# Gates and branch products with the activations stationary, runs of equal matmuls, and a transposed x and memory from the host, in a two-layer encoder

## The chip, the cores and the metric

The kernel runs on one core of one Trainium2 chip. The metric is the device time of one execution in microseconds (us), the median of the runs.

## The reference

Two post-norm layers on 256 tokens of width 1024, in fp32. One input projection of each token gives the parts of three attention branches (latent attention with low-rank queries and keys, differential attention, attention into 256 memory tokens) and three gates:

```python
h = x @ w_in[l]
c_q, c_kv, k_pe, dq, dk, dv, mq, gate_pre = jnp.split(h, splits, axis=-1)
o_mla = _mla_branch(...); o_diff = _diff_branch(...); o_mem = _mem_branch(mq, mem, mem_w_kv[l])
g = jax.nn.sigmoid(gate_pre.reshape(b, s, N_BRANCH, d) + b_gate[l])
merged = (g[:, :, 0] * (o_mla @ wb[:512]) + g[:, :, 1] * (o_diff @ wb[512:1536])
          + g[:, :, 2] * (o_mem @ wb[1536:]))
x = _layernorm(DEEPNORM_ALPHA * x + merged @ w_out[l], ln1_g[l], ln1_b[l])
f = jnp.square(jax.nn.relu(x @ mlp_w1[l])) @ mlp_w2[l]
x = _layernorm(DEEPNORM_ALPHA * x + f, ln2_g[l], ln2_b[l])
```

## The kernel before

Every fp32 operand of a product is kept as a high and a low part in a reduced fp32 format (`F32R`). `mm3` (L119) makes a product of three matmuls, high x high, high x low, low x high. Where the moving operand is short (256 tokens), `mm_wide` (L124) does it in two: one with the high weights, which moves the high and the low part of the activations together (2 x 256 columns, a "wide" step), and one with the low weights and the high activations (256 columns, a "narrow" step); it alternates them k by k. `wload` (L98) loads a weight tile into a ring of 6 raw buffers on SP's queue and splits it: a cast on ACT (L111, the high part) and a subtraction on DVE (L112, the low part) into a ring of 8 tiles (`whl`). `evac` (L136) does the same to a result in PSUM. PSUM has 8 banks: four under the name `acc`, four under `sm`.

At the start x is loaded with the tokens on the partitions, transposed by TensorE in blocks of 128 x 128 and split (`fill_xT`, L181), and then the first group of differential queries, keys and values is projected (`DiffProj.step`, L234). The memory is loaded and transposed likewise (`load_memT`, L278), once for each layer.

A layer is a list of steps in a string (`ORDER`, L52): P projects a differential group, D, M and A are attention heads of the three branches, L and U the latent path, T, K and Q memory and its queries; g, h, e are the gates of the memory, the differential and the latent branch, and G, H, E the branch products. A token such as `g0` advances that generator by one yield. A planner, which simulates the engines, then lays out the instructions of each engine, with the program's order as priority; it can pass an instruction that is not ready, and takes tiles from the rings as they come free.

`gate` (L650) computes 256 output features of one gate: two weight tiles, 128 features stationary, 256 tokens moving, 8 k x 3 matmuls for each 128 features into one half of an `acc` bank, then tanh on ACT with the bias as a per-partition scalar (L667). `branch` (L672) does the same for a branch product, with 4 or 8 k; its result is multiplied by the gate (L695, L697) and added to the merged sum (L698), and after the last branch the sum is split into the stationary tiles `mhl` of the product with w_out (L701, L702). So the merged sum is made with features on the partitions, as the product with w_out (L899) needs it. After w_out comes a layer norm, then the MLP: `mlp1` (L930, mm_wide) and the second product (`mlp2_mm`, L963, mm3 with the activations stationary and 512 columns of weights moving).

Of the kernel before, what the change touches and what calls it, by code (L numbers as in the profile page):

```python
# [17 lines left out]
P = 128  # L18
T = 256
# [24 lines left out]
BUFS = dict(raw=6, whl=8, whlx=4, att=12, o=6, pexp=4, natd=3, gt=4, fr=2, pT=2, sc=8)  # L44
# [15 lines left out]
def encoder_trunk(ctx: ExitStack, tc: tile.TileContext, x, mem, positions, w_in, b_gate,  # L60
                  q_norm, kv_norm, w_uq, w_ukv, lam, subln, w_mkv, w_branch, w_out,
                  ln1_g, ln1_b, w1, w2, ln2_g, ln2_b, inv, rows, out):
# [35 lines left out]
    def wload(src, a, b, ring="whl"):  # L98
# [25 lines left out]
    def mm_wide(ps, lh, ll, r2, first, last):  # L124

        if last:
            PE.matmul(ps[:, 0, :], lhsT=ll, rhs=r2[:, 0, :], start=False, stop=False)
        PE.matmul(ps, lhsT=lh, rhs=r2, start=first, stop=last)  # L128
        if not last:
            PE.matmul(ps[:, 0, :], lhsT=ll, rhs=r2[:, 0, :], start=False, stop=False)  # L130
# [69 lines left out]
    class DiffProj:  # L200
# [13 lines left out]
        def queries_keys(self, t, cs=range(4)):  # L214
# [4 lines left out]
            for c in cs:  # L219
                w = self.weights(0, c)  # L220
                for k in range(2 * c, 2 * c + 2):
                    xh, xl = xk(self.xT, k, t)
                    mm3(self.qk[t], xh, xl, w[0][:, k % 2], w[1][:, k % 2], k == 0, k == KD - 1)
# [819 lines left out]
```

## Time and profile before

| what | value |
|---|---|
| median of 3 runs | 1015.45 us (1015.1 to 1015.85) |
| the profiled execution | 1014.8 us |
| its span in the trace | 1013.0 us |
| matmuls on PE | 6277 |

The profile is of one execution. PE is TensorE's matmuls, PEld its weight loads, DVE, ACT and POOL the other engines, SP the engine that issues most DMAs; a "q" behind an engine's name is its sequencer, which issues DMAs. L120 is line 120 of the kernel. A group of instructions is named by line, engine, operation and tiles, out<-in. Matmuls are pipelined: each shows some 0.28 to 0.4 us, though the next starts much earlier, so the distance between two starts tells more than a duration. Idle time of an engine is given with what ended it.

### The profile page before, as it was taken

How to read it: one execution, taken by the hardware profiler on the slowest of the kernel's cores; microseconds unless marked ns; L12 is line 12 of the kernel's file. 1: busy time of each engine (PE TensorE's matmuls, PEld its weight loads, DVE VectorE, ACT ScalarE, POOL GpSimd, SP SyncE). 2: the span in 40 equal slices, each digit the busy share in tenths (PEclk: the TensorE clock that was granted, in tenths of full speed). 3: DMA queues.
4: the chain of work that ended last, by engine and by line, in shares of the span. 5: the costliest groups of instructions: out<-in, count | busy, mean ns of one | idle time of the engine just before them, and what ended most of it. 6: DMA issues, size and time to landing. Idle time of an engine off the chain costs nothing.

```text
span 1013.0 us, 16430 instructions
## 1 busy us (share of the span) xinstructions
PE 997.7 (98%) x6277; PEld 903.6 (89%) x6277; DVE 741.8 (73%) x1135; ACT 590.2 (58%) x1078; POOL 44.3 (4%) x86
## 2 busy tenths in 40 slices
PE   7999999999999999999999999999999999999997
PEld 6989899999998888888889989999999978888885
DVE  6868789677769776665776888887677876656664
ACT  6767777666564554444634877776665625444540
POOL 0101010000000000000000210000100000000000
PEclk9999999999999999999999999999999999999999
DMA  9776554545667366666754754455356725766631
GB/s 330 229 211 169 144 146 139 153 122 149 242 185 239 108 204 192 194 192 190 252 160 145 230 167 141 136 157 146 107 164 231 247 85 158 233 191 180 204 116 41
DMA packets 133258, 178.06 MB, mean 176 GB/s; under 512 B 6528, under 2 KB 115132, under 8 KB 133180
## 3 DMA queue, kind: packets, MB, share of 16 engines
q1 hardware_dynamic: 132203, 176.22, 57.1%
q8 instruction: 49, 0.80, 0.3%
q10 hardware_dynamic: 976, 0.80, 0.2%
q14 instruction: 30, 0.24, 0.1%
HBM read 174.89 MB, written 2.10 MB: 175 GB/s over the span
## 4 chain that ended last, share of the span: by engine, by line
PE 95%; DVE 2%; DMA 2%; ACT 1%; issue 1%; DVEq 0%; ACTq 0%
PE mlp1.sm L128 11%; PE branch.acc L121 6%; PE branch.acc L122 6%; PE branch.acc L120 6%; PE mlp2.acc L120 6%; PE mlp2.acc L122 6%; PE mlp2.acc L121 6%; PE mlp1.sm L130 5%; PE diff_proj.acc L120 5%; PE diff_proj.acc L121 5%; PE diff_proj.acc L122 5%; PE diff_att.sm L515 2%; PE mq.acc L128 1%; PE gate.acc L121 1%; PE gate.acc L120 1%; PE gate.acc L122 1%
## 5 line engine op out<-in xcount | busy, mean ns | idle before, releaser
L112 DVE TENSOR_TENSOR mlp1.whl<-mlp1.raw,mlp1.whl 128x1024 fp32r<-128x1024 f32 x124 | 150.9, 1224 | 86.7 <-ACT mlp1.whl L111 83.4
L111 ACT CAST mlp1.whl<-mlp1.raw 128x1024 fp32r<-128x1024 f32 x124 | 129.5, 1051 | 90.6 <-PE mlp2.acc L122 43.0
L128 PE MATMUL mlp1.sm<-wout.xT,mlp1.whl 128*128 128x512 f32 x480 | 167.0, 398 | 0.0
L130 PE MATMUL mlp1.sm<-wout.xT,mlp1.whl 128*128 128x256 f32 x420 | 117.8, 281 | 0.0
L128 PEld LDWEIGHTS mlp1.sm<-wout.xT,mlp1.whl 128*128 128x128 f32 x480 | 87.1, 188 | 16.8
L120 PE MATMUL mlp2.acc<-mlp1.whl,mlp1.att 128*128 128x512 f32 x240 | 93.5, 389 | 0.0
L122 PE MATMUL mlp2.acc<-mlp1.whl,mlp1.att 128*128 128x512 f32 x240 | 93.4, 389 | 0.0
L121 PE MATMUL mlp2.acc<-mlp1.whl,mlp1.att 128*128 128x512 f32 x240 | 93.4, 389 | 0.0
L112 DVE TENSOR_TENSOR branch.whl<-branch.raw,branch.whl 128x1024 fp32r<-128x1024 f32 x56 | 68.3, 1220 | 26.5 <-ACT branch.whl L111 26.1
L130 PEld LDWEIGHTS mlp1.sm<-wout.xT,mlp1.whl 128*128 128x128 f32 x420 | 79.3, 189 | 2.5
L111 ACT CAST branch.whl<-branch.raw 128x1024 fp32r<-128x1024 f32 x56 | 58.8, 1051 | 32.8 <-PE branch.acc L122 19.7
L112 DVE TENSOR_TENSOR diff_proj.whl<-diff_proj.raw,diff_proj.whl 128x1024 fp32r<-128x1024 f32 x51 | 62.1, 1219 | 14.2 <-ACT diff_proj.whl L111 13.9
L111 ACT CAST diff_proj.whl<-diff_proj.raw 128x1024 fp32r<-128x1024 f32 x51 | 53.9, 1061 | 17.6 <-PE diff_proj.acc L122 9.0
L533 ACT COPY mlp1.sum<-mlp1.sm 128x256 f32<-128x256 f32 x60 | 22.4, 373 | 57.6 <-PE mlp1.sm L128 57.6
L121 PEld LDWEIGHTS mlp2.acc<-mlp1.whl,mlp1.att 128*128 128x128 f32 x240 | 45.1, 188 | 9.5
L122 PEld LDWEIGHTS mlp2.acc<-mlp1.whl,mlp1.att 128*128 128x128 f32 x240 | 45.1, 188 | 9.4
L120 PEld LDWEIGHTS mlp2.acc<-mlp1.whl,mlp1.att 128*128 128x128 f32 x240 | 45.1, 188 | 8.8
L120 PE MATMUL diff_proj.acc<-diff_proj.whl,mlp1.xT 128*128 128x512 f32 (+1 forms) x128 | 44.1, 345 | 0.5 <-ACT mlp1.xT L138 0.5
L121 PE MATMUL diff_proj.acc<-diff_proj.whl,mlp1.xT 128*128 128x512 f32 (+1 forms) x128 | 43.3, 339 | 0.0
L122 PE MATMUL diff_proj.acc<-diff_proj.whl,mlp1.xT 128*128 128x256 f32 (+1 forms) x128 | 43.2, 341 | 0.0
L120 PE MATMUL diff_proj.acc<-diff_proj.whl,start.xT 128*128 128x512 f32 (+1 forms) x124 | 42.3, 343 | 0.0
L121 PE MATMUL diff_proj.acc<-diff_proj.whl,start.xT 128*128 128x256 f32 (+1 forms) x124 | 41.7, 339 | 0.1
(444 smaller groups left out, 2909.8 us busy)
## 6 DMA issues: line engine op xcount, KB each, us to landing
mlp1.raw<-in_mlp_w_dram SPq DMA_DIRECT2D x124, 512.0 KB, 4.5
branch.raw<-in_w_branch_dram SPq DMA_DIRECT2D x32, 512.0 KB, 3.5
diff_proj.raw<-in_w_in_dram SPq DMA_DIRECT2D x62, 256.0 KB, 3.3
branch.raw<-in_w_in_dram SPq DMA_DIRECT2D x24, 512.0 KB, 3.7
diff_proj.raw<-in_w_in_dram SPq DMA_DIRECT2D x20, 512.0 KB, 3.8
wout.raw<-in_w_out_dram SPq DMA_DIRECT2D x16, 512.0 KB, 3.6
gate.raw<-in_w_in_dram SPq DMA_DIRECT2D x12, 512.0 KB, 3.7
mem_keys.raw<-in_mem_w_kv_dram SPq DMA_DIRECT2D x8, 512.0 KB, 7.1
```

What stands on the lines that cost most here:

```text
L111: S.copy(out=hl[:, 0, :n], in_=raw[:, :n])
L112: V.tensor_tensor(hl[:, 1, :n], raw[:, :n], f32v(hl[:, 0, :n]), ALU.subtract)
L120: PE.matmul(ps, lhsT=lh, rhs=rh, start=start, stop=False)
L121: PE.matmul(ps, lhsT=lh, rhs=rl, start=False, stop=False)
L122: PE.matmul(ps, lhsT=ll, rhs=rh, start=False, stop=stop)
L128: PE.matmul(ps, lhsT=lh, rhs=r2, start=first, stop=last)
L130: PE.matmul(ps[:, 0, :], lhsT=ll, rhs=r2[:, 0, :], start=False, stop=False)
L515: PE.matmul(po[:, t * T:(t + 1) * T], lhsT=pT[:, hl, kt * T + t * P:kt * T + (t + 1) * P], rhs=vh[:, :, kt * T + j * P:kt * T + (j + 1) * ...
L533: S.copy(out=d, in_=ps[:, 1, :])
```

## The change

- `gate` and `branch` take 512 output columns (n = 0 or 1) instead of 256. The activations, 128 tokens at a time, are stationary and 512 columns of weights move; each uses two `acc` banks, one per token half, and one weight tile of two k and 512 columns per step. A gate has four steps (yields), a branch two (memory), four (differential) or two and a third for transposes (latent).
- The result has tokens on the partitions. So the gate's bias is loaded as a broadcast to all partitions into one of two buffers (on SP's queue, at the gate's first step) and added by DVE before the tanh, and the merged sum is transposed by TensorE and evacuated into `mhl`.
- `mm_wide` does a whole chain of eight k: four wide steps, eight narrow ones, four wide ones.
- The host hands in x and memory transposed too. x comes in five pieces on ACT's queue and is split from SBUF; each piece is followed by its steps of the first projection. Memory comes in two pieces with tiles of its own (`mT`).
- The order strings are new and differ for the two layers. Three pairs of gate tiles instead of four single ones.

```diff
+    "L0 T0 L0 P0 Q0 P0 K0 L0 K0 D0 K0 D0 Q0 M0 M1 P1 M0 D0 P1 M0 P2 M0 P1 D0 D0 M1 D0 P1 M1 P2 U0 P2 U0 "
+    "M1 D1 P2 D0 D1 P3 e0 P3 D1 D2 P3 D1 P3 D2 D1 D2 D1 D3 g0 D2 D3 D1 A2 D2 g0 A0 D2 D2 D3 g0 e0 g0 A2 "
+    "A0 e0 e0 D3 A1 g1 A0 D3 A0 D3 A1 D3 g1 A2 A1 g1 H1 g1 A1 A3 A0 A2 G0 h1 A1 h0 G0 A3 h1 H1 h0 A3 A2 "
+    "A3 h1 G1 H1 A3 G1 h1 H0 e1 e1 E0 H1 H0 H0 h0 h0 e1 H0 E0 E1 e1 E1 E0 E1",
+    "L0 K0 P0 L0 P0 Q0 K0 L0 D0 Q0 D0 D0 M0 K0 T0 M0 U0 D0 D0 D0 M0 P1 P1 U0 P1 P1 D0 M0 P2 D1 D1 D1 M1 "
+    "P2 D1 P2 D1 M1 e0 P2 P3 P3 D1 D2 D2 M1 P3 D2 M1 e0 D2 P3 D1 D2 D2 D3 A0 D2 D3 D3 A1 e0 e0 g1 g0 D3 "
+    "A3 A0 A0 g1 A0 g0 D3 D3 D3 g1 A0 g0 g0 A1 A2 A1 A2 A3 A1 g1 A1 G1 h0 A2 A3 A2 h0 A3 G1 A2 h1 h1 G0 "
+    "h1 h0 H1 A3 G0 H0 h0 h1 H1 H1 H1 H0 H0 e1 E0 H0 e1 E0 E1 e1 E0 e1 E1 E1",
...
+        def both(k):
+            PE.matmul(ps, lhsT=ws[k // 4][0][:, k % 4, sl], rhs=r2(k), start=k == 0, stop=k == KD - 1)
+
+        def low(k):
+            PE.matmul(ps[:, 0, :], lhsT=ws[k // 4][1][:, k % 4, sl], rhs=r2(k)[:, 0, :], start=False, stop=False)
+
+        for k in range(4):
+            both(k)
+        for k in range(KD):
+            low(k)
+        for k in range(4, KD):
+            both(k)
...
+        for h in range(2):
+            raw = wp.tile([P, 4, T], F32, tag="raw", bufs=BUFS["raw"], name=nm("memr"))
+            nc.sync.dma_start(out=raw, in_=wsrc(mem_t, 4 * h, 4, 0, T))
+            m = act.tile([P, 2, 4, T], F32R, tag="mT", bufs=2, name=nm("mT"))
+            split(m[:, 0], m[:, 1], raw)
+            mT.append(m)
...
+    for k0, nk in ((0, 1), (1, 1), (2, 2), (4, 2), (6, 2)):
+        raw = wp.tile([P, nk, T], F32, tag="raw", bufs=BUFS["raw"], name=nm("x0"))
+        nc.scalar.dma_start(out=raw, in_=wsrc(x_t, k0, nk, 0, T))
+        xh, xl = (xT[k0 // 4][:, s, k0 % 4:k0 % 4 + nk, :] for s in range(2))
+        split(xh, xl, raw)
+        for t in range(2):
+            first.queries_keys(t, range(k0, k0 + nk))
     for t in range(2):
+        first.values(t)
...
+        def gate(i, n):
+
+            bias = free_bias.pop(0)
+            nc.sync.dma_start(out=bias, in_=b_gate[l, i, n * 512:(n + 1) * 512].partition_broadcast(P))
+            pgs = [acc_tile() for _ in range(2)]
+            for c in range(4):
+                if c > 0:
+                    yield
                 stage[0] = "gate"
+                wh, wl = wload(wsrc(wi, 2 * c, 2, O_G + i * D + n * 512, 512), 2, 512)
+                for k2 in range(2):
+                    k = 2 * c + k2
+                    for t in range(2):
+                        xh, xl = xk(xT, k, t)
+                        mm3(pgs[t], xh, xl, wh[:, k2], wl[:, k2], k == 0, k == KD - 1)
+            gts = free_gates.pop(0)
+            for t in range(2):
+                V.tensor_tensor(gts[t], pgs[t], bias, ALU.add)
+                S.activation(gts[t], gts[t], AF.Tanh, scale=0.5)
+            free_bias.append(bias)
+            gates[i, n] = gts
...
+                        mm3(pbs[t], o[k // 2][:, 0, ts], o[k // 2][:, 1, ts], wh[:, k2], wl[:, k2],
+                            k == 0, k == nk - 1)
...
+            for t in range(2):
+                gt, m = gts[t], merged[t][:, n * 512:(n + 1) * 512]
+                if i == 2:
+                    V.scalar_tensor_tensor(m, gt, 1.0, pbs[t], ALU.add, ALU.mult)
+                    continue
+                V.scalar_tensor_tensor(gt, gt, 1.0, pbs[t], ALU.add, ALU.mult)
+                V.tensor_tensor(m, m, gt, ALU.add)
+            if i > 0:
+                return
+            yield
             stage[0] = "branch"
+            for t in range(2):
+                ps = sm_tile()
+                for a in range(4):
+                    c = n * 512 + a * P
+                    PE.transpose(ps[:, a * P:(a + 1) * P], merged[t][:, c:c + P], ident)
+                for h in range(2):
+                    mv = mhl[2 * n + h].rearrange("p s (a q) -> p s a q", a=2)
+                    ts = slice(t * P, (t + 1) * P)
+                    evac(mv[:, 0, :, ts], mv[:, 1, :, ts],
+                         ps[:, h * T:(h + 1) * T].rearrange("p (a q) -> p a q", a=2), scale=0.5)
```

## Rows read from the trace of the kernel before

**Rows 1.** The page: engine, busy us (share of the span), instructions.

```profile
PE 997.7 (98%) x6277; PEld 903.6 (89%) x6277; DVE 741.8 (73%) x1135; ACT 590.2 (58%) x1078; POOL 44.3 (4%) x86
```

**Rows 2.** The page: the chain that ended last, by engine.

```profile
PE 95%; DVE 2%; DMA 2%; ACT 1%; issue 1%; DVEq 0%; ACTq 0%
```

**Rows 3.** Waits of PE: total us, times, longest us; first and last of six.

```profile
PE start.sm L186 <- DMA start.x<-in_x_dram: 5.3, 2, 4.3
...
PE mlp1t.sm L120 <- ACT wout.xT L138: 0.2, 1, 0.2
```

**Rows 4.** Timeline of PE (start us, us, instruction): 24 consecutive gate starts, first and last.

```profile
253.49 0.28 PE L121 MATMUL gate.acc<-start.xT,gate.whl 128*128 128x256 f32 x1
...
256.25 0.28 PE L120 MATMUL gate.acc<-start.xT,gate.whl 128*128 128x256 f32 x1
```

**Rows 5.** Timeline of PE: 11 starts of a projection, 22 of the second MLP product.

```profile
542.77 0.39 PE L120 MATMUL diff_proj.acc<-diff_proj.whl,mlp1.xT 128*128 128x512 f32 x1
...
545.06 0.39 PE L121 MATMUL diff_proj.acc<-diff_proj.whl,mlp1.xT 128*128 128x512 f32 x1
...
420.04 0.40 PE L120 MATMUL mlp2.acc<-mlp1.whl,mlp1.att 128*128 128x512 f32 x1
...
424.81 0.39 PE L120 MATMUL mlp2.acc<-mlp1.whl,mlp1.att 128*128 128x512 f32 x1
```

**Rows 6.** Timeline of PE: joints of the mm_wide chains in mlp1.

```profile
411.35 0.63 PE L128 MATMUL mlp1.sm<-wout.xT,mlp1.whl 128*128 128x512 f32 x2
...
414.16 0.63 PE L128 MATMUL mlp1.sm<-wout.xT,mlp1.whl 128*128 128x512 f32 x2
414.63 0.28 PE L130 MATMUL mlp1.sm<-wout.xT,mlp1.whl 128*128 128x256 f32 x1
...
416.99 0.63 PE L128 MATMUL mlp1.sm<-wout.xT,mlp1.whl 128*128 128x512 f32 x2
```

**Rows 7.** Timeline of PE: four transposes among matmuls.

```profile
269.23 0.60 PE L843 MATMUL mla_att.sm<-consts,uq.nat 128*96 128x128 f32 x4
...
269.78 0.28 PE L121 MATMUL branch.acc<-diff_att.o,branch.whl 128*128 128x256 f32 x1
```

**Rows 8.** Timeline of PE at the start: first steps of the projection, and the next work after it.

```profile
8.85 0.78 PE L120 MATMUL diff_proj.acc<-start.whl,start.xT 128*128 128x512 f32 x1
9.42 0.63 PE L121 MATMUL diff_proj.acc<-start.whl,start.xT 128*128 128x512 f32 x1
...
11.13 0.63 PE L122 MATMUL diff_proj.acc<-start.whl,start.xT 128*128 128x512 f32 x1
...
27.90 0.28 PE L413 MATMUL diff_proj.sm<-consts,prow 60*128 60x60 f32 x1
```

**Rows 9.** A stretch at the start: busy us of each engine (instructions), PE clock, DMA share, GB/s.

```profile
8.80:12.30 3.50, 3.38 (x9) 2.22 (x7) 3.22 (x8) 2.72 (x4) 0.00 (x0) 1.00 0.97 311
```

**Rows 10.** Groups of ACT: busy us, mean ns of one, idle before.

```profile
L111 ACT CAST diff_proj.whl<-diff_proj.raw 128x1024 fp32r<-128x1024 f32 x51 | 53.9, 1061 | 17.6 <-PE diff_proj.acc L122 9.0 <-DMA diff_proj.raw<-in_w_in_dram 4.6 <-PE mq.acc L130 2.1
L667 ACT ACTIVATE consts<-branch.acc,consts 128x256 f32<-128x256 f32 x24 | 10.1, 475 | 2.9 <-PE branch.acc L122 2.9
```

**Rows 11.** A group of DVE, the same columns.

```profile
L697 DVE SCALAR_TENSOR_TENSOR consts<-consts,branch.acc 128x512 f32<-128x512 f32 x16 | 10.9, 681 | 2.4 <-PE branch.acc L122 2.3
```

**Rows 12.** A stretch of the first layer's attention part, columns as in rows 9.

```profile
100.00:200.00 100.00, 100.00 (x728) 94.57 (x727) 81.43 (x138) 72.93 (x163) 8.11 (x19) 1.00 0.51 145
```

**Rows 13.** Timeline of PE before the product with w_out, first layer.

```profile
304.98 1.69 PE L291 MATMUL load_memT.sm<-consts,load_memT.memn 128*128 128x128 f32 x14
...
308.78 0.50 PE L122 MATMUL load_memT.acc<-wout.whl,branch.att 128*128 128x512 f32 x1 [0.73 <-DVE branch.att L702]
```

**Rows 14.** SP's queue: w_out's issues, gate loads (KB, us to landing), a parameter load.

```profile
272.74 23.70 SPq L109 DMA_DIRECT2D wout.raw<-in_w_out_dram  x8
gate.raw<-in_w_in_dram SPq DMA_DIRECT2D x12, 512.0 KB, 3.7
262.83 0.42 SPq L578 DMA_DIRECT2D branch.lnp<-in_ln_g_dram  x1
```

More of the change, by code (lines that the diff above doesn't have):

```diff
@@ L122, in mm3, with mm_wide @@
         PE.matmul(ps, lhsT=ll, rhs=rh, start=False, stop=stop)
[L124 to L130, printed above, removed]
+    def mm_wide(ps, ws, sl, r2):
+        def both(k):
[8 more added lines that the diff above has]
+            both(k)
     def halves(pool_tile):
@@ L164, in encoder_trunk @@
     junk = carve(512)
-    free_gates = [carve(512) for _ in range(BUFS["gt"])]
+    free_gates = [[carve(512) for _ in range(2)] for _ in range(BUFS["gt"])]
+    free_bias = [carve(512) for _ in range(BUFS["gb"])]
     ident = carve(P)
@@ L218, in queries_keys @@
                 self.qk[t] = acc_tile()
[L219 to L223, printed above, removed]
+            for k in ks:
+                nk = 1 if len(ks) == 1 else 2
+                w = self.weights(0, k - k % nk, nk)
+                xh, xl = xk(self.xT, k, t)
+                mm3(self.qk[t], xh, xl, w[0][:, k % nk], w[1][:, k % nk], k == 0, k == KD - 1)
         def values(self, t):
@@ L229, in values @@
             for k in range(KD):
[L230 removed]
+                w = self.weights(1, k - k % 4, 4)
                 xh, xl = xk(self.xT, k, t)
@@ L337, in encoder_trunk @@
     first = DiffProj(0, 0, xT)
-    for t in range(2):
-        x0 = wp.tile([P, D], F32, tag="raw", bufs=BUFS["raw"], name=nm("x0"))
-        for h in range(2):
-            hs = slice(h * 512, (h + 1) * 512)
-            (nc.sync, nc.scalar)[h].dma_start(out=x0[:, hs], in_=x[0, t * P:(t + 1) * P, hs])
-        fill_xT(xT, x0, t)
-        if t == 0:
-            queues[:] = [nc.sync, nc.scalar]
-            first.weights(0, 0)
-            queues[:] = [nc.sync]
-    for t in range(2):
-        first.step(t)
+    for k0, nk in ((0, 1), (1, 1), (2, 2), (4, 2), (6, 2)):
[5 more added lines that the diff above has]
+            first.queries_keys(t, range(k0, k0 + nk))
+    for t in range(2):
+        first.values(t)
     pos_i = init.tile([P, 2], I32, name="pos_i")
@@ L938, in mlp1 @@
                     ps = halves(sm_tile)
[L939 to L942 removed]
+                    mm_wide(ps, ws, slice(jj * P, (jj + 1) * P), lambda k: xk2(xT, k))
                     add_halves(fr[:, jj * T:(jj + 1) * T], ps)
@@ L1030 @@
     data.append(("rows", _np.concatenate([_np.asarray(inputs[n]).reshape(-1, P) for n in _ROWS])))
+    data += [(n + "_t", _np.ascontiguousarray(_np.asarray(inputs[n])[0].T)) for n in ("x", "mem")]
     for name, a in data:
```

150 lines of the change are left out of this document (45 added, 105 removed).

## The prediction, made before the changed kernel was run

> **What bounds the kernel now.** I read the engine totals first, then the chain that ended last, then the waits of TensorE, and only then single instructions. TensorE is busy for 997.7 of 1013.0 us, DVE for 73% and ACT for 58% [rows 1]; the chain that ended last is PE for 95% [rows 2]. Matmuls overlap in the trace, so busy time alone proves little. The view of PE's waits decides: its six rows sum to 7.5 us, 5.3 of them for x at the start [rows 3]. So this kernel is a queue of matmuls without holes, and an edit is worth what it takes out of the distance from one matmul's start to the next (the pitch). DVE, ACT and DMA matter only where they open a hole. The profiled execution took 1014.8 us, 0.65 under the median of the runs shown (1015.45); the sum is made against 1014.8 and 0.65 is added at its end.
>
> **Gates and branches: 256 columns become 512.** Before, weights are stationary and 256 tokens move. Per layer the gates are 3 x 8 output tiles x 8 k x 3 = 576 matmuls and the branches 8 tiles x (4+8+4) k x 3 = 384; for two layers 1152 and 768. After, 128 tokens are stationary and 512 weight columns move: 576 and 384. The 24 starts from 253.49 to 256.25 give 2.76/23 = 0.120 us for 256 columns [rows 4]. For 512 columns there are two rows with the same roles: the projection from the same xT, eleven starts from 542.77 to 545.06, 2.29/10 = 0.229 us; and the second MLP product, 22 starts from 420.04 to 424.81, 4.77/21 = 0.2271 us [rows 5]. Gates resemble the first: 1152 x 0.120 - 576 x 0.229 = 138.2 - 131.9 = 6.3 us. Branches resemble the second: 768 x 0.120 - 384 x 0.2271 = 92.2 - 87.2 = 5.0 us. Together -11.3 us. The ends, if both run at 0.229 or both at 0.2271, are -10.5 and -12.4.
>
> The Trainium skill speaks against this term. Its page "TensorE: Matmul & The Clock Gate", section "Back-to-back issue gap", gives a warm gap of columns / 2.4 ns plus about 2.5 ns, so that two matmuls of 256 cost only 2.5 ns more than one of 512. By that the term would be an estimated 960 x 2.5 ns = 2.4 us. The rows do not agree: 0.120 x 2 - 0.229 leaves 11 ns.
>
> **mm_wide in runs.** It serves mlp1 (60 chains of 8 k), mq and mem_keys (8 each): 76 chains. Seven of eight wide steps now alternate with a 256-column step; after, four wide, eight narrow, four wide. From 411.35 to 416.99 two chains take 5.64 us, 2.82 each. Where two wide steps follow each other today, at the joint of two chains, they take 0.47 us together, 0.235 each [rows 6]. So I do not find that alternation is what costs: the wide step moves two pieces of 256, and is dearer than 0.2271 in either order. With 8 x 0.235 = 1.88 the eight narrow steps share 0.94, 0.1175 each when a wide step follows, against 0.120 among themselves [rows 4]. After: 1.88 + 7 x 0.120 + 0.1175 = 2.8375 us, 0.0175 more; x 76 = +1.3 us. The other end takes wide steps in a run at 0.2271: 2.774 us, x 76 = -3.5. I take +1.3, since its row has the same operands.
>
> **Transposes.** Four of them take, from 269.23 to the second matmul behind them at 269.78, 0.55 us less one ordinary step of 0.12: 0.43, so 0.108 each [rows 7]. Removed are 16 for x and 2 x 16 for the memory; added are 4 per token half, column half and layer for the merged sum, 32. Memory against merged is 32 x 0.108 on both sides: 0. x's belong to the start.
>
> **The start.** Today PE waits 4.3 us for x [rows 3], which is turned and split, and the projection runs from 8.85 until the next work at 27.90: 19.05 us for 48 steps of 512 and 48 of 256. Those are worth 48 x 0.229 + 48 x 0.120 = 16.8; the first starts lie 1.71/4 = 0.4275 apart, which is 1.2 columns per ns, the lower level of the clock (the clock column of that stretch says 1.00 all the same); eight steps lie before the clock rises, 1.6 us dearer, and the rest is waiting [rows 8, 9]. After, the first matmul needs 128 KB of x and 256 KB of weights: 384 KB where PE waits today for the 512 KB of x's first half, so 128 KB or 0.4 us less at the 311 GB/s at which the queues flow [rows 9]: about 4.0. Then two casts: 0.475 for 256 columns at most, and 0.53 for 512, half the 1.06 of 1024 [rows 10]. First matmul at about 5.1; + 16.8 + 1.6 + 0.3 for waits = 23.8; gain 27.9 - 23.8 = 4.1 us. Does the data keep up? x and weights are 4 MB, 4/0.311 = 12.9 us; even counted from 4.0 that is 16.9, before PE's 23.8. The casts of one pair of k take ACT 1.06 + 0.53, under the 12 x 0.229 = 2.7 of PE. Ends: 2.0, if the later x loads, which wait on ACT's queue for a free raw buffer, hold ACT's casts behind them; 5.0, if the clock rises earlier.
>
> **What lies beside PE.** 24 bias additions of 512 columns cost DVE 24 x 0.68 = 16.4 us; the 48 tanh of 256 columns take ACT 0.475 each, half as many twice as wide cost no more [rows 10, 11]. DVE is busy 81% from 100 to 200 [rows 12], and these 16 us spread over two attention parts of some 270 us: +3 points, cover remains, cost 0. If it were gone, each late drain would cost PE the 0.68 of one operation. The merged evacuations become 16 of 256 instead of 8 of 512 (the same columns); memory and x splits replace equal ones: 0. Weight bytes and the number of splits stay; rows of 2 KB replace rows of 1 KB.
>
> **The join before w_out.** Today PE waits 0.73 us there for the last operation on the merged sum, after 14 memory transposes filled the time before [rows 13]. After, the chain is two drains, additions, transposes, casts: 2 x 0.68 + 2 x 0.68 + 8 x 0.108 + about 1.2 = 4.8 us behind the last branch step, but the first four k of w_out, 48 x 0.2271 = 10.9 us, need only the first column half. I put 0; ends -0.7 per kernel and +1.5 (twice 0.73) if the order places these transposes too early.
>
> **Sum.** 1014.8 - 11.3 + 1.3 + 0 - 4.1 = 1000.7; + 0.65 = 1001.35, rounded to 1001.
>
> **Rivals.**
> *The bias load stalls the weight queue.* Each gate first issues a bias load on SP's queue, into one of two buffers. If the buffer's last user has not been added yet, SP waits, and all weight loads behind it wait. The order string opens a gate one 2.7 us step after the gate that frees its buffer closes at two places: e1 after h1 in layer 0, g0 after e0 in layer 1. Price: 2 x 0.68 of additions [rows 11] + 0.42 to issue + 3.7 for the weights [rows 14] + 1.06 cast [rows 10] = 6.5, less 2.7 cover = 3.8 each, 7.6 us: 1009. For it: such a load is not held behind the weights of its stretch, as the norms' parameters are. Against: SP runs far ahead, w_out's loads start at 272.74 [rows 14] for matmuls behind 304.98 [rows 13], and the planner can pass a blocked load. Chance 0.12.
> *512 columns cost 0.235 here too,* as in the wide steps: 230.4 - 960 x 0.235 = 4.8 us instead of 11.3: 1008. Against it are both rows of 0.227 to 0.229. Chance 0.04. The page's rule above would lead still higher, to an estimated 1010.
> *Everything falls well:* runs at 0.2271 (-3.5), start -5: 1014.8 - 11.3 - 3.5 - 5 + 0.65 = 996 (995.65). Chance 0.10.
> *PSUM banks, slower.* A gate or branch now holds two of the four acc banks through 2 to 4 steps, and the order string has up to five such units open at once. A unit that opens waits for another's drain, 2 x 0.68 = 1.36 us if no ready matmul lies between. The 24 units decide against the change from 14.1/1.36 = 11 uncovered openings; all 24 would give 1001.35 + 32.6 = 1034. Against: today's order already slips other steps between two matmuls of one product [rows 7]. Chance 0.05.
> *The gain is spent exactly,* within 0.2%: 0.02.
>
> **How the numbers follow.** Forecast 0.67: 1001, own range 997.5 to 1004.5 from the ends above. Range 995 to 1008, taking in the good case and the edges of the first two rivals. A difference under about 0.2% (2 us) cannot be told from none here. Faster 0.93, same 0.02, slower 0.05.
>
> **What would show it.** 6277 - 960 - 48 + 32 = 5301 matmuls. Gate pitch 0.229, branch 0.227. In mlp1, W-W pitch of 0.235 inside a run would bear out the +1.3; 0.227 refutes it. The projection should start near 5.1 and end near 23.8. PE waits over 3 us behind a bias load show the first rival; waits on DVE drains of acc at openings the fourth. I am wrong if PE's waits outside the start exceed some 5 us.

## The result and the profile of the changed kernel

The changed kernel takes 1003.06 us (median of 4 runs, 1002.75 to 1004.25) against 1015.28 of the kernel before on the same chip (4 runs, 1014.77 to 1015.85): a ratio of 0.9882 with a 95% interval of 0.9865 to 0.9899. The forecast was 1001, its own range 997.5 to 1004.5. The profiled execution took 1002.75 us with a span of 1001.0, 12.0 less than the 1013.0 of before.

The page of the changed kernel: the span, busy us by engine, and the chain that ended last.

```profile
span 1001.0 us, 14551 instructions
...
PE 983.9 (98%) x5301; PEld 850.0 (85%) x5301; DVE 753.8 (75%) x1164; ACT 587.2 (59%) x1060; POOL 45.6 (5%) x86
...
PE 90%; DVE 4%; DMA 3%; issue 2%; ACT 1%; POOL 0%; DVEq 0%; ACTq 0%
```

Against [rows 1] PE issues 976 matmuls less, exactly the 5301 worked out. DVE does 12 us more work; outside the start PE waits 0.8 us for it, against 1.5 before. In [rows 2] PE held 95% of the chain, now 90%: DVE, DMA and ACT have 8% instead of 5%, so the last thing that released the work is more often another engine. Where, the waits of PE say (us in total, times, longest).

```profile
PE diff_proj.sm L413 <- DMA prow<-in_rows_dram: 2.6, 1, 2.6
PE diff_proj.acc L129 <- ACT diff_proj.whl L122: 2.3, 1, 2.3
PE diff_proj.acc L130 <- DVE diff_proj.whl L123: 2.2, 2, 1.6
PE mlp1t.sm L565 <- DVE mlp1t.fr L538: 0.6, 1, 0.6
PE load_memT.acc L129 <- ACT branch.att L158: 0.5, 1, 0.5
```

The first wait stands at a small transpose of the norms' rows that now comes ahead of any data, and costs nothing: x is not there either. The other two large ones are in the first projection; the rest of the kernel has waits of 0.6 us and less. PE's timeline of the changed kernel gives the pitches (start us, us, instruction; xN joins N in a row):

```profile
5.09 1.22 PE L129 MATMUL diff_proj.acc<-diff_proj.whl,start.xT 128*128 128x512 f32 x2 [2.29 <-ACT diff_proj.whl L122]
...
7.89 0.79 PE L130 MATMUL diff_proj.acc<-diff_proj.whl,start.xT 128*128 128x512 f32 x1 [1.57 <-DVE diff_proj.whl L123]
...
11.45 0.79 PE L130 MATMUL diff_proj.acc<-diff_proj.whl,start.xT 128*128 128x512 f32 x1 [0.63 <-DVE diff_proj.whl L123]
...
199.57 0.39 PE L129 MATMUL gate.acc<-branch.whl,diff_att.o 128*128 128x512 f32 x1
...
200.48 0.40 PE L130 MATMUL gate.acc<-branch.whl,diff_att.o 128*128 128x512 f32 x1
...
402.42 1.12 PE L140 MATMUL mlp1.sm<-wout.xT,mlp1.whl 128*128 128x256 f32 x8
403.38 2.00 PE L137 MATMUL mlp1.sm<-wout.xT,mlp1.whl 128*128 128x512 f32 x8
405.22 1.12 PE L140 MATMUL mlp1.sm<-wout.xT,mlp1.whl 128*128 128x256 f32 x8
...
408.01 1.11 PE L140 MATMUL mlp1.sm<-wout.xT,mlp1.whl 128*128 128x256 f32 x8
...
700.75 0.40 PE L129 MATMUL branch.acc<-gate.whl,mlp1.xT 128*128 128x512 f32 x1
...
705.31 0.39 PE L131 MATMUL branch.acc<-gate.whl,mlp1.xT 128*128 128x512 f32 x1
```

Read them by the weight's name behind the arrow: the tile's own name is only that of the stage that happened to be open. Between 700.75 and 705.31 stand 21 gate starts, 4.56/20 = 0.228 us each; between 199.57 and 200.48 five branch starts, 0.91/4 = 0.2275. Forecast were 0.229 and 0.2271. A chain of mm_wide takes 5.59/2 = 2.795 us from one group of eight narrow steps to the next but one; before it was 2.82 [rows 6]. Eight wide steps in a run fill 405.22 - 403.38 = 1.84 us, 0.23 each, not 0.235.

Where the 12.0 us came from, read off PE's timelines as the distances between the first and last matmuls of a stage (the last column is the fastest version, from the experiments):

| stage (us) | before | after | difference | x interleaved |
|---|---|---|---|---|
| start to last step of the first projection | 27.69 | 28.06 | +0.4 | 26.13 |
| to the first step of w_out, first layer | 278.74 | 270.96 | -7.8 | 271.32 |
| w_out, first layer | 22.66 | 23.12 | +0.5 | 23.06 |
| MLP, first layer | 178.56 | 177.71 | -0.85 | 177.71 |
| to the first step of w_out, second layer | 270.71 | 265.42 | -5.3 | 265.25 |
| w_out, second layer | 21.56 | 22.81 | +1.25 | 22.82 |
| MLP, second layer | 161.25 | 160.60 | -0.65 | 160.59 |
| behind the last matmul | 7.95 | 8.38 | +0.4 | 8.0 |

The steps between w_out and the MLP are equal within 0.04. So the gain lies where the gates and branches are, a little in the MLP, and the start brought nothing. Its cause is on DVE and on the queues of ACT and SP (timelines of the changed kernel, where the brackets give the idle time before an instruction and what ended it; then waits of SP's queue up to 12 us):

```profile
3.33 0.46 ACTq L343 DMA_DIRECT2D diff_proj.x<-in_x_t_dram  x1
...
7.03 0.17 DVE L358 CAST consts<-pos_i 128x2 f32<-128x2 int32 x1 [2.86 <-DMA pos_i<-in_positions_dram]
7.14 0.69 DVE L123 TENSOR_TENSOR diff_proj.whl<-diff_proj.raw,diff_proj.whl 128x512 fp32r<-128x512 f32 x1
...
9.50 0.38 DVE L361 TENSOR_SCALAR consts<-consts 128x24 f32<-128x24 f32 x2 [1.33 <-DMA consts<-in_inv_freq_dram]
...
SPq L111 <- DMA pos_i<-in_positions_dram: 2.2, 1, 2.2
SPq L111 <- DVE diff_proj.whl L123: 0.8, 1, 0.8
```

The cast of the token positions, 256 numbers that nothing needs for a long time, stands on DVE ahead of the subtraction of the first weights and waits 2.86 us for its 1 KB. The weights' upper part had been cast by about 5.0; their lower part begins at 7.14, and PE has its second kind of step only at 7.89. The next instruction of the same chain, at 9.50, waits 1.33 us for the frequencies (12 KB), ahead of the second weights, for which PE waits at 11.45. SP's queue, which brings the weights, stands as well: 2.2 us until the positions have landed and 0.8 us until DVE's subtraction of the first weights is done.

### The profile page after: what moved, and what is told of

Read it like the earlier page. It is cut to its first block, busy times and chain, and to the rows that moved or that the text cites. A ratio compares the mean times of both kernels' runs of the same rounds, so it can differ in the third digit from the quotient of the medians.

```text
span 1001.0 us, 14551 instructions
## 1 busy us (share of the span) xinstructions
PE 983.9 (98%) x5301; PEld 850.0 (85%) x5301; DVE 753.8 (75%) x1164; ACT 587.2 (59%) x1060; POOL 45.6 (5%) x86
## 4 chain that ended last, share of the span: by engine, by line
PE 90%; DVE 4%; DMA 3%; issue 2%; ACT 1%; POOL 0%; DVEq 0%; ACTq 0%
PE mlp1.sm L137 11%; PE mlp1.sm L140 6%; PE mlp2.acc L129 6%; PE mlp2.acc L131 6%; PE mlp2.acc L130 6%; PE diff_proj.acc L130 5%; PE diff_proj.acc L131 4%; PE diff_proj.acc L129 4%; PE branch.acc L129 2%; PE branch.acc L130 2%; PE branch.acc L131 2%; PE gate.acc L129 2%; PE gate.acc L130 2%; PE gate.acc L131 2%; DMA load_memT.memr<-in_mem_t_dram 2%
## 5 line engine op out<-in xcount | busy, mean ns | idle before, releaser
L137 PE MATMUL mlp1.sm<-wout.xT,mlp1.whl 128*128 128x512 f32 x480 | 122.5, 392 | 0.0
L137 PEld LDWEIGHTS mlp1.sm<-wout.xT,mlp1.whl 128*128 128x128 f32 x480 | 86.2, 189 | 15.2
L123 DVE TENSOR_TENSOR diff_proj.whl<-diff_proj.raw,diff_proj.whl 128x1024 fp32r<-128x1024 f32 (+1 forms) x49 | 58.8, 1201 | 17.9 <-ACT diff_proj.whl L122 17.3
L123 DVE TENSOR_TENSOR gate.whl<-gate.raw,gate.whl 128x1024 fp32r<-128x1024 f32 x48 | 58.4, 1221 | 18.0 <-ACT gate.whl L122 17.4
L140 PEld LDWEIGHTS mlp1.sm<-wout.xT,mlp1.whl 128*128 128x128 f32 x480 | 65.5, 190 | 4.7
L140 PE MATMUL mlp1.sm<-wout.xT,mlp1.whl 128*128 128x256 f32 x480 | 66.9, 282 | 0.0
L122 ACT CAST diff_proj.whl<-diff_proj.raw 128x1024 fp32r<-128x1024 f32 (+1 forms) x49 | 50.9, 1038 | 21.4 <-PE diff_proj.acc L131 12.0
L122 ACT CAST gate.whl<-gate.raw 128x1024 fp32r<-128x1024 f32 x48 | 50.4, 1052 | 17.8 <-PE diff_proj.acc L131 5.8
L123 DVE TENSOR_TENSOR branch.whl<-branch.raw,branch.whl 128x1024 fp32r<-128x1024 f32 x32 | 39.1, 1222 | 14.8 <-ACT branch.whl L122 14.4
L122 ACT CAST branch.whl<-branch.raw 128x1024 fp32r<-128x1024 f32 x32 | 33.6, 1051 | 27.0 <-PE gate.acc L131 12.2
L130 PE MATMUL diff_proj.acc<-diff_proj.whl,start.xT 128*128 128x512 f32 (+1 forms) x128 | 44.7, 349 | 2.2 <-DVE diff_proj.whl L123 2.2
L129 PE MATMUL diff_proj.acc<-diff_proj.whl,start.xT 128*128 128x512 f32 (+1 forms) x128 | 43.8, 351 | 2.3 <-ACT diff_proj.whl L122 2.3
L131 PE MATMUL diff_proj.acc<-diff_proj.whl,start.xT 128*128 128x512 f32 (+1 forms) x128 | 44.4, 347 | 0.0
```

What stands on the lines that cost most here:

```text
L122: S.copy(out=hi, in_=src)
L123: V.tensor_tensor(lo, src, f32v(hi), ALU.subtract)
L129: PE.matmul(ps, lhsT=lh, rhs=rh, start=start, stop=False)
L130: PE.matmul(ps, lhsT=lh, rhs=rl, start=False, stop=False)
L131: PE.matmul(ps, lhsT=ll, rhs=rh, start=False, stop=stop)
L137: PE.matmul(ps, lhsT=ws[k // 4][0][:, k % 4, sl], rhs=r2(k), start=k == 0, stop=k == KD - 1)
```

## The experiments

Times of before on these chips are 1015.16 (first four runs), 1015.37 (the next four) and 1015.17 (the last three). "After" below is the changed kernel, 1003.06, which was timed with before at 1015.28. Totals 1 us apart are not told apart by these runs; such readings rest on the stages of the profiles. No kernel here leaves out work.

### The start: which queue holds it

The theory: instructions that stand in order on DVE and ACT, not the amount of data, hold the start. The rival: the loads cannot come sooner.

**Positions' cast later,** held on DVE's list behind the last subtraction of the first query and key projection (`x_split`).

```diff
-    V.tensor_copy(pos_f, pos_i)
+    with tc.issue_after(x_split):
+        V.tensor_copy(pos_f, pos_i)
```

> The changed kernel, with one edge added: the cast of the token positions on DVE (and with it the chain that makes the rotation tables) is queued behind the last split of the first query and key projection. Theory (DVE queue): in the changed kernel this cast waits 2.86 us for the 1 KB of positions that land at 7.0, and the first weight subtraction, ready at about 5.0, stands behind it; so PE's second kind of matmul begins at 7.89. Expected: that step at about 6.0, the projection's end 2 to 4 us before 28.06, the kernel at 999 to 1001.5 against 1003.06. Rival (supply): the pieces of x and weights come late in any case (ACT's casts wait for DMA up to 13.7), the end moves by under 0.7 and the kernel stays above 1002.3. Rival (clock): steps start earlier but the 0.43 us distance lasts to about 15 us all the same; gain about 1.

1002.41 us (1001.62 to 1003.81), ratio 0.9876. PE's second kind of step starts at 6.12 instead of 7.89, but the next wait takes most of this back, and the projection ends at 27.52 instead of 28.06. Timelines of this kernel:

```profile
3.34 0.46 ACTq L343 DMA_DIRECT2D diff_proj.x<-in_x_t_dram  x1
...
8.35 0.62 ACT L122 CAST start.xT<-diff_proj.x 128x512 fp32r<-128x512 f32 x1 [2.99 <-DMA diff_proj.x<-in_x_t_dram]
8.87 0.61 ACT L122 CAST diff_proj.whl<-diff_proj.raw 128x512 fp32r<-128x512 f32 x1
...
9.54 1.22 PE L129 MATMUL diff_proj.acc<-diff_proj.whl,start.xT 128*128 128x512 f32 x2 [1.51 <-ACT diff_proj.whl L122]
```

ACT issues the third piece of x at 3.34, behind other work, then stands 2.99 us at that piece's cast, and the cast of weights that PE needs stands behind it. The wait on DVE was real, but ACT's was right behind it. An end 0.54 us earlier and a time above 1002.3 are the figures of the first rival, supply, and this run does not exclude it: that piece of x lands 5 us after its issue.

**All small loads later,** in addition: the loads of positions and frequencies behind the last piece of x on ACT, that of the norms' rows behind the first projection's weights on SP.

```diff
-    nc.scalar.dma_start(out=inv_b, in_=inv[0].partition_broadcast(P))
+    with tc.issue_after(x_load):
+        nc.scalar.dma_start(out=inv_b, in_=inv[0].partition_broadcast(P))
...
-    nc.sync.dma_start(out=prow, in_=rows)
+    with tc.issue_after(w_load):
+        nc.sync.dma_start(out=prow, in_=rows)
```

> As the kernel with the positions' cast behind the splits, and also the loads of positions and frequencies behind the last piece of x on ACT's queue, and the load of the norm rows behind the first projection's weights on SP's queue. Theory (DVE queue alone): within 0.5 us of that kernel. Rival (issue order of the loads): x's third piece, issued at 3.33 behind the positions' load, and the first weights, issued at 1.21 behind the norm rows, come 0.4 to 1.5 us earlier, and the kernel is another 0.5 to 1.5 us faster, at 998 to 1000.

1003.37 us (1002.49 to 1003.81), 0.9882: no gain. The planner filled the freed first place on SP's queue with a gate's bias load of 256 KB, issued at 0.72; x's first piece landed at 5.51 instead of 2.85, the first matmul started at 7.33 and the projection ended at 28.90. The run tested something else than it was meant to; with 256 KB in front, the first matmul came 2.2 us later than in the run before.

**The x load alone, in the kernel before** (x transposed by the host, projection in pieces, all else as before).

```diff
-        fill_xT(xT, x0, t)
+        nc.scalar.dma_start(out=raw, in_=wsrc(x_t, k0, nk, 0, T))
+        S.copy(out=xh, in_=raw)
+        V.tensor_tensor(xl, raw, f32v(xh), ALU.subtract)
```

> The kernel before with nothing changed but the start: x transposed by the host, loaded in five pieces on ACT's queue, the projection interleaved with the pieces. Theory (DVE queue): the same block by the positions' cast stands here, and the start gives at most 1 us: 1014.3 to 1015.7. Rival (prediction): 4.1 us faster, 1011.2, if the block is an effect of the new order and does not stand here.

1016.6 us (11 runs), ratio 1.001 [1.0001, 1.0018]: slower, if by little, which neither expectation had. The first matmul is at 5.17, the last of the projection at 28.20 (27.69 before). Sixteen transposes less and a start 3.7 us earlier came to nothing, as in the changed kernel. DVE waits 0.99 us for the positions here, and then, in its timeline,

```profile
9.20 0.38 DVE L359 TENSOR_SCALAR consts<-consts 128x24 f32<-128x24 f32 x2 [3.02 <-DMA consts<-in_inv_freq_dram]
```

3.02 us for the frequencies, with the second weights behind it. The block stands here too, at another load of the same chain.

**x in a buffer of its own, four of its five pieces on SP's queue behind the weights, positions' cast later.**

```diff
+    xraw = act.tile([P, KD, T], F32, tag="mT", bufs=2, name="xraw")
     for k0, nk in pieces:
-        raw = wp.tile([P, nk, T], F32, tag="raw", bufs=BUFS["raw"], name=nm("x0"))
-        nc.scalar.dma_start(out=raw, in_=wsrc(x_t, k0, nk, 0, T))
+        (nc.sync if k0 else nc.scalar).dma_start(out=xraw[:, k0:k0 + nk, :], in_=wsrc(x_t, k0, nk, 0, T))
+        raw = xraw[:, k0:k0 + nk, :]
```

> The changed kernel with three edits at its start: x lands in a buffer of its own (the memory's, free until then) instead of the shared raw ring; four of its five pieces are loaded on SP's queue, each behind the weights of the piece before, and only the first on ACT's; and the cast of the positions stands on DVE behind the last subtraction of x. Theory (in-order queues: DVE's wait for the positions, and x loads that stand behind casts on ACT, cost the start what the forecast had gained): nothing but data and PE is left; 384 KB land by about 4, then 1.2 us per 384 KB at 311 GB/s, the last piece by about 12.7. First matmul near 5.1, no PE wait over 1 us behind it, last projection matmul near 24 to 24.5 (28.06 in the changed kernel, 23.8 forecast), kernel 999 to 999.5. Rival (supply: the queues cannot bring 3 MB in time, whatever the order): PE waits on casts whose loads land later than this arithmetic, projection ends at 26 or later, 1001 or more. Second rival (the gain is given back behind the projection, since the latent weights or the rotary tables come late): projection ends near 24, but the latent work waits, and the kernel stays at 1002 to 1003.

1000.39 us (4 runs, 1000.05 to 1001.52), ratio 0.9855 [0.984, 0.987]: the fastest version. Its runs lie below all of the changed kernel's, though the two intervals against before still touch. The time lies between the two expectations; the end of the projection, 26.13, is in the range of the rival, supply (26 or later). The first matmul starts at 4.70, and DVE's subtractions wait for nothing but casts. What is left are loads that land late: PE waits 1.48 and 0.53 us for the third weights. Timelines of PE and ACT, then stretches (us; busy us of PE, PEld, DVE, ACT, POOL; clock; DMA share; GB/s), the last of them from the kernel before:

```profile
10.78 0.73 PE L129 MATMUL diff_proj.acc<-diff_proj.whl,start.xT 128*128 128x512 f32 x2 [1.48 <-ACT diff_proj.whl L122]
12.04 0.50 PE L130 MATMUL diff_proj.acc<-diff_proj.whl,start.xT 128*128 128x512 f32 x1 [0.53 <-DVE diff_proj.whl L123]
...
9.68 1.04 ACT L122 CAST diff_proj.whl<-diff_proj.raw 128x1024 fp32r<-128x1024 f32 x1 [1.02 <-DMA diff_proj.raw<-in_w_in_dram]
```

```profile
3.00:4.00 1.00, 0.00 (x0) 0.00 (x0) 0.00 (x0) 0.31 (x1) 0.00 (x0) 1.00 0.99 184
4.00:6.00 2.00, 1.30 (x3) 1.06 (x4) 1.12 (x2) 1.05 (x3) 0.00 (x0) 1.00 0.88 225
6.00:8.00 2.00, 2.00 (x6) 1.36 (x6) 1.12 (x2) 0.62 (x1) 0.00 (x0) 1.00 1.00 285
8.00:10.00 2.00, 1.30 (x6) 0.74 (x4) 0.69 (x1) 0.94 (x2) 0.00 (x0) 1.00 1.01 337
10.00:12.00 2.00, 0.73 (x2) 0.30 (x2) 1.24 (x2) 1.33 (x3) 0.00 (x0) 1.00 1.08 367
...
4.00:6.00 2.00, 1.65 (x8) 1.57 (x8) 0.00 (x0) 0.53 (x1) 0.00 (x0) 1.00 1.09 388
```

From 3 to 8 the DMA engines are busy 0.88 to 1.00 of the time, yet carry 184 to 285 GB/s, not the 311 of [rows 9]; 337 is reached after 8. The forecast's rate came from a stretch that begins at 8.80. The early time alone is not the reason, since the kernel before carried 388 GB/s from 4 to 6. Order has a part in it: SP's queue stands 0.7 us at 3.0 until x's first piece has landed, which came on ACT's queue. The rest is open.

**All of x issued at once on ACT's queue,** with the same buffer and cast.

```diff
+    for k0, nk in pieces:
+        nc.scalar.dma_start(out=xraw[:, k0:k0 + nk, :], in_=wsrc(x_t, k0, nk, 0, T))
     for k0, nk in pieces:
+        raw = xraw[:, k0:k0 + nk, :]
```

> As the run beside it (x in a buffer of its own, positions' cast behind the splits), but all five pieces of x are issued on ACT's queue at the beginning, none on SP's. Theory (in-order queues): ACT no longer issues x behind casts, so the long PE waits go; x and weights now flow together, 3 MB by about 9.7 + 1 us, but the casts of x stand ahead of those of the second and third weight piece on ACT, and each stands until its piece of x has landed. A PE wait of 1 to 2 us is left at the second or third weight piece; projection ends at 25 to 26, kernel 1000 to 1001. Rival (supply): the first weights land later since x takes half of the flow; first matmul at 6 or later, and the projection at 27 to 28, no gain.

1004.01 us (1002.37 to 1004.84), 0.9884 [0.9867, 0.99]: a miss of 3 us, with the rival's outcome (no gain) but not its reason, since the first matmul starts at 4.84. The third weights come 1.5 us later than in the run before (their second kind of step at 13.52, not 12.04): ACT casts the last pieces of x ahead of them and stands 2.37 us for one. And the hole is paid for twice. Stretches of this kernel, the same columns, and two starts of PE:

```profile
10.00:12.00 2.00, 0.57 (x2) 0.00 (x0) 1.38 (x2) 1.92 (x3) 0.00 (x0) 1.00 0.25 70
...
14.00:17.00 3.00, 3.00 (x10) 2.33 (x9) 1.50 (x2) 1.46 (x2) 0.00 (x0) 0.58 1.08 371
```

```profile
14.62 0.63 PE L131 MATMUL diff_proj.acc<-diff_proj.whl,start.xT 128*128 128x512 f32 x1
...
16.75 0.63 PE L131 MATMUL diff_proj.acc<-diff_proj.whl,start.xT 128*128 128x512 f32 x1
```

PE does 0.57 us of work from 10 to 12; from 14 to 17 the granted clock is 0.58 and the pitch 2.13/5 = 0.426 us, the lower of the two levels. The projection ends at 28.96, 2.83 behind the run before, of which 1.48 is the late weight and some 1.35 the clock.

### The order and the host's memory

**Runs undone** in the changed kernel (mm_wide alternating as before):

```diff
-        for k in range(4):
-            both(k)
         for k in range(KD):
-            low(k)
-        for k in range(4, KD):
+            if k == KD - 1:
+                low(k)
             both(k)
+            if k < KD - 1:
+                low(k)
```

> The changed kernel with mm_wide alternating wide and narrow steps again. Theory from the two traces: a chain in runs takes 2.795 us against 2.82, so undoing it costs 76 x 0.025 = 1.9 us: 1005.0. What the prediction held: a run is 0.0175 us dearer per chain, so undoing it gains 1.3 us: 1001.8. Wide-to-wide distance in a run 0.230, alternating pair 0.354.

1003.98 us (1003.92 to 1004.3), ratio 0.989. The two MLP stages are back at 178.56 and 161.35 us (before: 178.56 and 161.25), 1.6 more than in the changed kernel; in the total 0.9 of it shows, in part since this kernel's projection ended at 27.61, 0.45 earlier.

**Runs alone,** in the kernel before:

```diff
-                for k in range(KD):
-                    wh, wl = ws[k // 4]
...
+                mm_wide(ps, ws, slice(j * P, (j + 1) * P),
+                        lambda k: mT[k // 2][:, :, (k % 2) * T:(k % 2 + 1) * T])
```

> The kernel before with nothing changed but mm_wide, which does four wide, eight narrow, four wide steps. Theory: 76 x 0.025 = 1.9 us faster than before: 1013.4. What the prediction held: 1.3 us slower: 1016.6.

1013.56 us (11 runs), ratio 0.9987 [0.9978, 0.9996]: 1.6 less. The MLP stages are 177.71 and 160.59. In these stages the two runs give 1.6 and 1.5 us for 60 of the 76 chains, some 1.9 for all of them, where +1.3 was forecast.

**Plain order:** the changed kernel with an order string like that of before, units in rows one after the other, the same for both layers. It has two pairs of gate tiles instead of three, since three do not fit with that order; no wait of PE names one.

```diff
-    "L0 T0 L0 P0 Q0 P0 K0 L0 K0 D0 K0 D0 Q0 M0 M1 P1 M0 D0 P1 M0 P2 M0 P1 D0 D0 M1 D0 P1 M1 P2 U0 P2 U0 "
...
+    "P0 P0 T0 L0 L0 L0 K0 K0 K0 Q0 Q0 D0 D0 D0 D0 D0 D0 D0 U0 U0 M0 M0 M0 M0 P1 P1 P1 P1 D1 D1 D1 D1 D1 D1 D1
...
+     P3 P3 P3 P3 g0 g0 g0 g0 A0 A0 A0 A0 A0 G0 G0 D3 D3 D3 D3 D3 D3 D3 g1 g1 g1 g1 A1 A1 A1 A1 A1 G1 G1
...
+     H1 H1 H1 H1 e0 e0 e0 e0 e1 e1 e1 e1 E0 E0 E0 E1 E1 E1",
```

> The changed kernel with order strings in the manner of the kernel before: each gate and branch runs its steps in one piece, the same for both layers; two pairs of gate tiles instead of three, since three don't fit with this order. Theory (PE has no holes in either order): within 2 us of the changed kernel, 1003 to 1005. Rival (the new order is what hides drains and the bias loads): a gate's bias load finds its buffer in use at each second gate, and drains stand open: 5 to 12 us slower, 1008 to 1015, with PE waits on acc drains or weights in the attention part.

1026.75 us (4 runs), ratio 1.0112: 23.7 more than after, and slower than before. Waits and timeline of PE:

```profile
PE gate.acc L123 <- ACT mla_att.o L869: 4.3, 2, 2.2
PE branch.sm L702 <- DVE branch.merged L693: 3.2, 4, 1.3
...
PE mla_att.sm L854 <- DVE mla_att.pT L150: 1.8, 3, 1.1
```

```profile
304.03 0.80 PE L123 MATMUL gate.acc<-branch.whl,mla_att.o 128*128 128x512 f32 x1 [2.16 <-ACT mla_att.o L869]
...
305.05 0.63 PE L123 MATMUL gate.acc<-branch.whl,mla_att.o 128*128 128x512 f32 x1
305.48 0.63 PE L124 MATMUL gate.acc<-branch.whl,mla_att.o 128*128 128x512 f32 x1
```

Each of these waits is for an operand, none for a PSUM bank. The holes are at the end of each layer's attention part: nothing is left that could run while the last attention head is evaluated and while the merged sum is drained and transposed. Behind the hole the pitch is 0.43 us again. Behind the start and ahead of the MLPs, the waits sum to some 15 us of the 23.7. So the change needs an order like the interleaved one; that the pitch of the matmuls falls is not enough.

**The host's memory in the kernel before:**

```diff
-                    PE.transpose(ps[:, i * T + t * P:i * T + (t + 1) * P],
-                                 mn[t][:, k * P:(k + 1) * P], ident)
-            evac(mT[kk][:, 0, :], mT[kk][:, 1, :], ps)
+            nc.sync.dma_start(out=raw, in_=wsrc(mem_t, 4 * h, 4, 0, T))
+            S.copy(out=m[:, 0], in_=raw)
+            V.tensor_tensor(m[:, 1], raw, f32v(m[:, 0]), ALU.subtract)
```

> The kernel before with nothing changed but the memory, which the host hands in transposed (no transposes of it on TensorE, two tiles of its own). Theory: 32 transposes x 0.108 = 3.5 us leave PE's queue: 1011.8. Rival: they fill time that PE would wait at the join before w_out, so only the 16 of layer 0, or less, are gained: 1013.5 to 1015.

1017.27 us (10 runs), ratio 1.0023 [1.0014, 1.0032]: 1.9 slower with 32 transposes (3.5 us) less, which neither expectation had. Its waits of PE show two new ones; below them are DVE's timeline in this kernel and, last, in the kernel before:

```profile
PE diff_proj.acc L258 <- DVE diff_proj.natd L394: 3.1, 1, 3.1
PE branch.acc L120 <- ACT mla_att.o L858: 2.0, 1, 2.0
...
19.48 1.23 DVE L286 TENSOR_TENSOR load_memT.mT<-load_memT.memr,load_memT.mT 128x1024 fp32r<-128x1024 f32 x1
...
30.79 0.28 DVE L394 TENSOR_TENSOR diff_proj.natd<-diff_proj.natd,diff_proj.rope 128x128 f32<-128x128 f32 x1
...
24.63 0.28 DVE L405 TENSOR_TENSOR diff_proj.natd<-diff_proj.natd,diff_proj.rope 128x128 f32<-128x128 f32 x1
```

These 5.1 us are not holes that the transposes had filled: in both places the operands come later. At the first, DVE does two subtractions of the memory (L286) ahead of the last rotation tables and the latent weights, and the last step of the rotation that PE waits for begins at 30.79 instead of 24.63. At the second, casts and subtractions of w_out's weights come ahead of the last attention head, whose last product starts at 297.30 instead of 289.29. Behind the first hole the granted clock is 0.72 from 28 to 34, some 1.2 us dearer. Less the transposes and the wait of 0.7 at the join before w_out [rows 13], which is gone, that makes an estimated 2.1, against 1.7 in the span. All of the loss is in the first layer (281.41 instead of 278.74 to w_out, 21.56 instead of 22.66 in w_out); the second is as before.

**The memory turned by TensorE in the changed kernel:**

```diff
-            split(m[:, 0], m[:, 1], raw)
...
+                    PE.transpose(ps[:, i * T + t * P:i * T + (t + 1) * P],
+                                 mn[t][:, k * P:(k + 1) * P], ident)
+            evac(mT[kk][:, 0, :], mT[kk][:, 1, :], ps)
```

> The changed kernel with one part undone: the memory is loaded as it lies and turned by TensorE (32 transposes more), all else as changed, the order of the work included. Forecast's price of the transposes alone: 32 x 0.108 = 3.5 us, 1006.5. Theory (in the new order they also stand ahead of what the join before w_out waits for, as the run with gates and order alone showed: its layer-0 stages were 7.4 us longer): 1008 to 1011, with the loss in the first layer's attention and w_out and none in the second layer. Rival (they fill holes, as in the kernel before, where taking them out gained nothing): 1003 to 1004.

1010.61 us (1007.98 to 1011.51), ratio 0.9949 [0.9933, 0.9965]; its profiled execution took 1007.98, with a span of 1006.2. That is 5.2 over the changed kernel: 3.5 for the transposes, 1.0 at the start, where the projection ends at 29.03 (this time the frequencies hold DVE, 4.31 us, and PE waits 3.0), and the last 0.7 about the join before w_out, where PE waits 1.8 instead of 0.7. The loss is in the first layer, as expected. What the other 2.4 us between the two medians are was not traced; the run of 1007.98 has a mean granted clock of 0.997, that of 1011.51 one of 0.993, and 0.4% of the span, an estimated 4 us, would be enough. DVE's timeline at the start:

```profile
10.58 0.38 DVE L373 TENSOR_SCALAR consts<-consts 128x24 f32<-128x24 f32 x2 [4.31 <-DMA consts<-in_inv_freq_dram]
```

**Gates and order alone:** the changed kernel with x, memory and mm_wide as before.

```diff
-        nc.scalar.dma_start(out=raw, in_=wsrc(x_t, k0, nk, 0, T))
+        fill_xT(xT, x0, t)
...
-            split(m[:, 0], m[:, 1], raw)
+            evac(mT[kk][:, 0, :], mT[kk][:, 1, :], ps)
...
-        for k in range(4):
-            both(k)
```

> The changed kernel with three parts undone: x and memory loaded as before and transposed by TensorE, mm_wide alternating. What is left are the gates and branches with 512 columns, the merged sum's transposes and the order. Theory: 1015.28 - 11.4 + 32 x 0.108 = 1007.3. Rival (gains overlap, or 512 columns bring less): above 1009, or below 1006 if the order itself closes holes.

1013.21 us (12 runs), ratio 0.9979 [0.9971, 0.9987], 6 more than expected. The second layer's part to w_out is 265.39, the changed kernel's gain in full; the first layer's two stages are 274.45 and 27.01, 7.4 above it. The wait that grew, and the stretch behind it (clock, DMA share and GB/s last):

```profile
PE load_memT.acc L129 <- ACT branch.att L158: 3.1, 2, 2.2
...
304.00:308.00 4.00, 3.08 (x8) 2.37 (x8) 4.00 (x8) 1.66 (x4) 0.00 (x0) 0.57 0.94 332
```

w_out waits 3.1 us for the casts of the merged sum instead of 0.5, and behind these holes seven steps, from 305.06 to 308.08, take 3.0 us instead of 1.6, at a granted clock of 0.57. The transposes (3.5), 2.6 more of this wait and 1.4 of the clock make 7.5, against 7.4. Whether the transposes cause the wait is open: the 16 of the second memory layout stand in the same stretch, but come only from 313.81 on.

## Why the prediction was right, and where it was not

**Bound.** PE is a queue of matmuls before and after. The sum of the steps' changes of pitch gave the time; DVE's 12 us more of work (16.4 were put) cost nothing, as forecast, and PE's waits outside the start are 1.9 us, where more than 5 were to refute the forecast.

**Gates and branches** (-11.3): confirmed. With 0.228 and 0.2275 the same counts give 138.2 - 131.3 + 92.2 - 87.4 = 11.7. In the stages: a layer's gates and branches should bring 5.85, and its 16 merged transposes cost 1.7. In the second layer that is -4.15 against the measured -5.3 + 1.25 = -4.05. In the first, which also loses 32 memory transposes (3.5), it is -7.65 against -7.8 + 0.5 = -7.3. The rows carried this: the same operands at the same width had been in the trace of before. The Trainium skill's page "TensorE: Matmul & The Clock Gate", section "Back-to-back issue gap", from which an estimated 2.4 us would have followed, is not borne out: 2 x 0.120 - 0.228 is 12 ns per pair of steps, not 2.5. The same section gives a sustained spacing of about 131 ns for 512 columns with a weight load each; no stretch here comes near it. It gives 512/1.2 ns at the lower clock, and with that the 0.426 agrees.

**mm_wide in runs** (+1.3): wrong sign, -1.9 (76 x 0.025), shown from both sides by the runs undone and the runs alone. The step that failed took the 0.235 at the joint of two chains as the price of a wide step behind a wide step. In a run it is 0.23, and 1.84 + 0.955 = 2.795. Within the run from 403.38 the starts lie 0.233, 0.236, 0.228, 0.233, 0.230, 0.227, 0.227 and 0.226 apart, with the joint of two chains in fourth place. So it is not the joint that is dear, but the first steps behind narrow ones, and the only pair of before stood there. The range (-3.5 to +1.3) held the value, the choice within it was the wrong end.

**The start** (-4.1): the first matmul came at 5.09 where 5.1 was forecast, but the projection ended at 28.06, not 23.8; +0.4 instead of -4.1. Two terms failed. "0.3 for waits" measured 2.8 (1.95 before 7.89, 0.83 before 11.45): it looked at bytes and at ACT's total work, not at what stands in front of what, the positions and frequencies on DVE, the x loads behind casts on ACT, and SP's queue behind both. The bound named for it, 2.0, was too narrow, too. And the lower clock lasted 16 steps, to about 15.0, instead of eight: 3.2 us instead of 1.6. That the waits keep it there is not shown: with x up front twelve steps from 4.84 on, almost without a hole, all came at 0.427, with x interleaved it rose behind the eighth. The version with x interleaved gets 1.9 of the 4.3 us back; the rest is its two waits for the third weights.

**Memory against merged transposes** (0): right in this kernel, where undoing the removal costs 5.2 us in the profile, 3.5 of them the transposes. The same removal made the kernel before 1.9 us slower, by what it did to the order on ACT and DVE, so the price of the transposes alone does not give the term.

**The join** (0): 0.5 + 0.2 us of waits against 0.73 [rows 13]; right.

**The errors offset.** -11.7 - 1.9 + 0.4, and +0.4 behind the last matmul, make -12.8; measured are -12.0 in the span. The 0.8 left was not traced. Two misses, of 3.2 us one way and 4.5 the other, nearly cancelled: the median is 2 us over the forecast, while one term was off by more than twice that. That the total came this close is in part luck; the term that carries the change, the gates and branches, is not.

**Rivals.** The bias loads do hold SP's queue (12.3 us in eight waits, the longest 3.0), but no wait of PE stands behind one. The width at 0.235 fell with the pitch. "Everything well" failed at the start only; its run term was half true. The rival of PSUM banks named the right danger, an opening without other work, but the wrong resource: with the plain order it came true at 1026.75, not for want of banks, but because the last chains before w_out had nothing beside them. The changed order string, which the prediction hardly priced, keeps it away.

## What to carry to other kernels

Price a change of the matmuls' shape by starts of the same operands elsewhere in the trace, and check that the row stands where the change will (the first wide steps behind narrow ones are not those further on). Before a start-up gain is booked, write down for every engine the instructions in order up to the first full stage, the small casts and the DMA issues among them: one instruction that waits for 1 KB holds all behind it. Work that is taken away can change the order in which the other engines come to theirs, so its price depends on the order around it, and a change of order and a removal are to be tried together and apart.

## What the hardware showed that was not expected

- A hole of PE can be paid twice. With x up front, after 0.57 us of work from 10 to 12, the pitch of 512 columns went from 0.23 to 0.426 us for some three us (granted clock 0.58 from 14 to 17); behind the 2.16 us hole of the plain order and the 3.1 us hole with the host's memory (0.72 from 28 to 34) it fell as well. It did not behind the 2.0 us hole of that kernel (1.00 from 300 to 306), nor with x interleaved, after 0.73 us of work from 10 to 12. What tells these apart is not shown.
- In the first microseconds the clock's column says 1.00 while the pitch is 0.427; there the pitch is the witness, not the column.
- The load of 1 KB of positions, issued at 2.84 on ACT's queue, let DVE go at 7.01: 4.2 us, no less than the pieces of x of 256 KB beside it (3.33 to 7.57).
- DMA engines that are busy 99% of a microsecond may carry 184 GB/s at the start and 337 five microseconds later, with loads of x and weights in both; the kernel before carried 388 from 4 to 6.
